# Three feed-forward stages: the down product of the last group of chunks by seven products of half size, and the next norm's blocks in the order in which they are finished

## The chip, the core and the metric

The kernel runs on one core of a Trainium2 chip. The metric is the device time of one execution in microseconds. Time before: 1751.9 us, the median of three runs (1751.84 to 1753.63).

The engines as the profile names them: PE multiplies matrices and accumulates into PSUM, PEld loads its weights, DVE and ACT work elementwise, POOL issues some of the DMAs (those that add to memory on chip among them), and SP issues the loads of the weights. Each engine has one queue of instructions and waits on semaphores of the others.

## The reference

A trunk of two layers on 512 tokens of width 1024, float32. Each layer is a feed-forward net, a mixer (gated linear attention, GLA, in the first layer, stick-breaking attention, SB, in the second) and another feed-forward net, each behind an RMSNorm:

```python
def swiglu(h, w_gate, w_up, w_down):
    return (jax.nn.silu(h @ w_gate) * (h @ w_up)) @ w_down

    for i in range(DEPTH):          # 2
        x = x + 0.5 * swiglu(rmsnorm(x, ffn1_norm[i]), ffn1_w_gate[i], ffn1_w_up[i], ffn1_w_down[i])
        h = rmsnorm(x, mix_norm[i])
...
        x = x + y.astype(x.dtype)
        x = x + 0.5 * swiglu(rmsnorm(x, ffn2_norm[i]), ffn2_w_gate[i], ffn2_w_up[i], ffn2_w_down[i])
    return rmsnorm(x, final_norm)
```

The gate and up matrices are 1024 x 2816, the down matrix is 2816 x 1024. So there are six stages in a row: FFN, GLA, FFN, FFN, SB, FFN, and then the last norm.

## The kernel before

**Layout.** The activations are held transposed: eight tiles `xs[0]` to `xs[7]` of 128 features x 512 tokens (in the traces all of them are `x`, in the order of instructions `x_81` to `x_88`). Float32 products are made of three matmuls: each operand is split into a high part (a cast to fp32r, on ACT) and a low part (the difference, on DVE), and PE adds high x high, low x high and high x low. So every weight block costs a cast (`wh`, L152), a subtraction (`wl`, L153) and, for PE, three matmuls for each pair of blocks. A matmul has 128 x 128 weights and 512 columns (tokens), or 256 where products are of half size.

**Seven products.** From chunk 2 on, gate and up products (`FFN.seven`) split weights and activations into 2 x 2 blocks and compute the product in Winograd's form: seven products of half size for eight, with sums of weight blocks (`sums_12`, `sums_34`, on DVE), sums of activation blocks (`t1` to `t4`) and sums of the results. `seven_down` does the same for the down product of a group of two chunks: the weights are 512 x 1024, taken in two parts; part 0 has the output blocks 0, 1 (lower) and 4, 5 (upper), part 1 the blocks 2, 3 and 6, 7. For each part it loads two blocks of 512 KB (`rawd`, two buffers) and queues two entries. `body_1` makes four products (with `b11`, `t1`, `t2`, `b21`), `body_2` three (`t3`, `b22`, `t4`); each product is 2 x 6 matmuls of 256 columns into the tiles `ps_w`, `ps_z` and `ps_q`. The weight sums `s34` of the second entry are split by `low_34` (casts at L427, low parts at L430). A result is added to half a tile of `xs` as soon as it is there (`add`, L418), three halves' results one over the other, so that `xs` is read and written 12 times in a part. The plain `down` (L334) takes 512 x 256 of the weights in an entry, 24 matmuls of 512 columns, and adds whole tiles (L367).

**Groups.** A stage has eleven chunks of 256 hidden features in six groups: `GROUPS = ((0, 2), (2, 4), (4, 6), (6, 8), (8, 9), (9, 11))`. While the gate and up products of a group run, the down products of the group before are mixed in between: for groups 1 and 3 (`DOWN_SEVEN`) by `seven_down`, its first part behind the first up product, its second part (`late`) some slots later; for the others by `down`. Some blocks of the plain downs are not added by DVE: ACT writes half the result to `d` (L362), and POOL starts a DMA that adds it to `xs` (L363). In group 4 these are six of eight blocks (`HOMES`). The down products of the last group, group 5, stand alone at the end of the stage: this part is called the tail here.

**Hidden values.** When an up product is done, the gated value is closed: `close` casts it whole and takes its low part (`hh`, `hl`); for a group in `DOWN_SEVEN` `close_first` and `close_second` make the halves `b11`, `b21`, `b22` and the four sums `t1` to `t4`, with a cast and a low part for each; places for some are free halves of the normed input `self.n`.

**The next norm.** In the tail each `xs[k]` gets its last sum, and `prep(k)` then makes the next stage's input from it: the high part `xh` (L544, ACT), the low part `xl` (L545, DVE), the square (L535, ACT) and the sum of the squares (L536, DVE). The scale of the norm is put on later, so PE can start the next stage's products on `xh` and `xl` before it is known; `new_norm` says in which order they take the eight blocks.

**What sets the order.** Work is queued as entries (`Feed.q`). An entry's weights are split when it is one of the next three and four tiles of full size are not yet taken; raw blocks are loaded up to six entries ahead, as far as their buffers go. The scheduler then orders each engine's instructions by priority; a queue is worked off in that order.

## Time and profile before

| | |
|---|---|
| median of three runs | 1751.9 us (1751.84 to 1753.63) |
| the profiled execution: time | 1752.18 us |
| the profiled execution: span, first to last instruction | 1750.2 us |
| granted TensorE clock, mean | 0.999 |
| matmuls | 12698 |
| tails of the three stages, PE, us from the span's start | 312.67 to 333.39; 850.83 to 871.55; 1172.27 to 1192.99 |
| weights loaded by SP in one 512 KB block (`rawd`), issue to landing | 3.8 us, median of 84 |

Times in the views are in us from the start of the span. A row of the timeline has the start, the duration, the engine, the line, the operation and its tiles, and then the idle time of the engine before it and what ended it. Rows of a window have, for each engine, the busy time and in brackets how many instructions it touches; then the granted clock, the mean share of the 16 DMA engines and GB/s. A row of the waits has the waiting instruction, what it waited for, the sum, how often, and the longest. Durations of neighbours overlap a little, since an instruction starts before the one before it on its engine has ended; how long a queue takes is read from start to start.

### The profile page before, as it was taken

Reading aid. Unit: us, or ns where it says so; the run is one execution under the profiler, and the core shown is the slowest. Engines: PE = TensorE matmul, PEld = TensorE weight load, DVE = VectorE, ACT = ScalarE, POOL = GpSimd, SP = SyncE. Lnnn points to the kernel's source line nnn. Section 1 sums busy time; section 2 is a strip of 40 time slices with the busy share of each in tenths; the row PEclk is TensorE's granted clock in tenths of the full one; section 3 lists DMA queues with packets and bytes.
Section 4 is the critical chain, followed back from the end, with each engine's and each line's share of the span. In section 5 each row is a group of like instructions: output and inputs, shape, how many; then the busy total and the mean of one; then the engine's idle time right before and its main releaser. Section 6 shows DMA issues by size and latency. Waiting matters only on the chain.

```text
span 1750.2 us, 31332 instructions
## 1 busy us (share of the span) xinstructions
PE 1740.0 (99%) x12698; PEld 1628.1 (93%) x12698; DVE 1507.0 (86%) x2490; ACT 1026.3 (59%) x1832; POOL 55.8 (3%) x85
## 2 busy tenths in 40 slices
PE   9999999999999999999999999999999999999998
PEld 8999999889888899999989999999888889999997
DVE  8999798786888989889799988977999679998886
ACT  7556555554665565555665555555666655565555
POOL 0000000200000000000000000010000000000000
PEclk9999999999999999999999999999999999999999
DMA  5533434412223443444334334343212234434441
GB/s 169 157 109 121 127 116 139 120 55 75 72 75 119 112 129 112 118 129 125 105 125 127 115 118 124 121 111 108 75 59 73 73 97 133 123 107 123 119 140 60
DMA packets 186244, 193.11 MB, mean 110 GB/s; under 512 B 4786, under 2 KB 170980, under 8 KB 186100
## 3 DMA queue, kind: packets, MB, share of 16 engines
q1 hardware_dynamic: 177760, 175.91, 32.3%
q0 software_dynamic: 8096, 14.92, 4.7%
q8 instruction: 99, 1.62, 0.4%
q14 instruction: 45, 0.37, 0.1%
q10 hardware_dynamic: 244, 0.29, 0.0%
HBM read 175.11 MB, written 2.10 MB: 101 GB/s over the span
## 4 chain that ended last, share of the span: by engine, by line
PE 95%; DVE 4%; ACT 1%; issue 0%; DVEq 0%
PE ps_w L779 22%; PE ps_f L80 16%; PE ps_d L80 16%; PE ps_q L779 11%; PE ps_z L779 6%; PE ps_w L412 5%; PE ps_t L80 5%; PE ps_b L80 4%; PE ps_q L412 2%; PE ps_z L412 1%; PE ps_z L1484 1%; PE ps_oT L1546 1%; PE ps_T L1531 1%; PE ps_bt L80 1%; PE ps_S L80 1%; PE ps_o L80 1%
## 5 line engine op out<-in xcount | busy, mean ns | idle before, releaser
L153 DVE TENSOR_TENSOR wl<-raw,wh 128x1024 fp32r<-128x1024 f32 x241 | 255.4, 1060 | 40.5 <-ACT wh L152 39.6
L152 ACT CAST wh<-raw 128x1024 fp32r<-128x1024 f32 x241 | 222.1, 922 | 81.2 <-PE ps_f L80 34.3
L153 DVE TENSOR_TENSOR wl<-s,wh 128x1024 fp32r<-128x1024 f32 x160 | 195.3, 1221 | 66.2 <-ACT wh L152 65.3
L779 PE MATMUL ps_w<-th,wh 128*128 128x256 f32 x864 | 238.8, 276 | 0.0
L779 PE MATMUL ps_w<-tl,wh 128*128 128x256 f32 x864 | 237.6, 275 | 0.0
L779 PE MATMUL ps_w<-th,wl 128*128 128x256 f32 x864 | 237.6, 275 | 0.0
L152 ACT CAST wh<-s 128x1024 fp32r<-128x1024 f32 x160 | 168.7, 1054 | 6.0 <-DVE s L765 6.0
L779 PEld LDWEIGHTS ps_w<-th,wh 128*128 128x128 f32 x864 | 165.8, 192 | 0.5 <-ACT ps_z L807 0.2
L80 PE MATMUL ps_f<-xh,wh 128*128 128x512 f32 x432 | 166.0, 385 | 0.0
L779 PEld LDWEIGHTS ps_w<-tl,wh 128*128 128x128 f32 x864 | 165.9, 192 | 0.0
L779 PEld LDWEIGHTS ps_w<-th,wl 128*128 128x128 f32 x864 | 165.9, 192 | 0.0
L80 PE MATMUL ps_f<-xh,wl 128*128 128x512 f32 x432 | 164.0, 380 | 0.5 <-DVE wl L153 0.5
L80 PE MATMUL ps_f<-xl,wh 128*128 128x512 f32 x432 | 163.8, 379 | 0.0
L80 PE MATMUL ps_d<-hh,wh 128*128 128x512 f32 x416 | 157.8, 379 | 0.0
L80 PE MATMUL ps_d<-hl,wh 128*128 128x512 f32 x416 | 157.7, 379 | 0.0
L80 PE MATMUL ps_d<-hh,wl 128*128 128x512 f32 x416 | 157.7, 379 | 0.0
L153 DVE TENSOR_TENSOR wl<-rawd,wh 128x1024 fp32r<-128x1024 f32 (+1 forms) x100 | 96.2, 962 | 8.6 <-ACT wh L152 8.6
L807 ACT COPY ps_z<-ps_w 128x256 f32<-128x256 f32 x72 | 26.1, 362 | 117.9 <-PE ps_w L779 117.7
L363 POOL DMA_DIRECT2D x<-d x53 | 46.0, 912 | 1525.9 <-ACT d L362 1108.1
L80 PEld LDWEIGHTS ps_f<-xh,wl 128*128 128x128 f32 x432 | 81.8, 189 | 11.4 <-DVE wl L153 0.9
L80 PEld LDWEIGHTS ps_f<-xl,wh 128*128 128x128 f32 x432 | 81.7, 189 | 11.5
L80 PEld LDWEIGHTS ps_f<-xh,wh 128*128 128x128 f32 x432 | 81.7, 189 | 10.7
(355 smaller groups left out, 5355.8 us busy)
## 6 DMA issues: line engine op xcount, KB each, us to landing
raw<-in_ffn_w_gate_dram SPq DMA_DIRECT2D x43, 1024.0 KB, 5.5
raw<-in_ffn_w_up_dram SPq DMA_DIRECT2D x43, 1024.0 KB, 5.4
rawd<-in_ffn_w_down_dram SPq DMA_DIRECT2D x84, 512.0 KB, 3.8
x<-d POOLq DMA_DIRECT2D x53, 256.0 KB, 4.4
raw<-in_gla_w_in_dram SPq DMA_DIRECT2D x12, 1024.0 KB, 5.3
raw<-in_sb_w_in_dram SPq DMA_DIRECT2D x16, 512.0 KB, 3.7
raw<-in_gla_w_out_dram SPq DMA_DIRECT2D x4, 1024.0 KB, 5.0
raw<-in_sb_w_in_dram SPq DMA_DIRECT2D x4, 1024.0 KB, 5.1
```

The costliest lines, as they stand in the source:

```text
L80: st["pe"] = nc.tensor.matmul(ps, l, r, start=first, stop=last).ins
L152: nc.scalar.copy(h[:, k], part)
L153: nc.vector.tensor_tensor(out=l[:, k], in0=part, in1=h[:, k].bitcast(F32), op=ALU.subtract)
L363: nc.gpsimd.dma_start(xs[k], d, accum_op=ALU.add)
L412: st["pe"] = nc.tensor.matmul(ps, l_, r_, start=first and c + n == 0, stop=c == 1 and n == 2, skip_group_check=True).ins
L779: st["pe"] = nc.tensor.matmul(o, l_, r_, start=first and j + n == 0, stop=j == 3 and n == 2, skip_group_check=True).ins
L807: v["copied"] = nc.scalar.copy(z, w).ins
L1484: nc.tensor.matmul(o_, l_, r_, start=first, stop=last, skip_group_check=True)
L1531: nc.tensor.transpose(ps[:, c0 : c0 + P], ys[yb][:, yc + j * P : yc + (j + 1) * P], ident)
L1546: nc.tensor.matmul(po[e * 64 : e * 64 + 64, j * P : T], self.v[j][:, c : c + 64], self.wt[p, e][bk][:, c0 : c0 + n], start=j == 0, stop=j ...
```

## The change

In the three feed-forward stages that are not the last, group 5 joins groups 1 and 3: its down product is made by `seven_down`, both parts directly behind each other at the end of the stage. Its two chunks are closed by `close_first` and `close_second`; for the second, the sums `t3` and `t4` get a whole tile of the normed input. `seven_down` has a new argument `nxt`: behind the last add to a block it calls `prep` for it. Blocks are finished in the order 0, 1, 4, 5, 2, 3, 6, 7, and the next stage's products take them in this order (`st["order"]`). The second part of group 3's `seven_down` moves from the second to the first slot of group 5, where it stood behind the first up product and now stands behind the first gate product. The last stage keeps its old form.

```diff
-    def seven_down(pool, w, r0, hs, part):
+    def seven_down(pool, w, r0, hs, part, nxt=None):
...
             for m in range(2):
                 add(m, 0, 1, flat(qs[m]))
+                if nxt is not None:
+                    nxt(part * 2 + m)
             yield
             for m in range(2):
                 prod(ws[m], v["a2"], 2, m, "t4", False)
                 add(m, 1, 0, flat(ws[m]))
+                if nxt is not None:
+                    nxt(part * 2 + m + 4)
             yield
...
     def new_norm():
-        st["h"], st["l"], st["made"] = st["nh"], st["nl"], range(KD)
+        st["h"], st["l"], st["made"] = st["nh"], st["nl"], st.pop("order", range(KD))
...
-        DOWN_SEVEN = (1, 3)
+        DOWN_SEVEN = (1, 3, 5)
...
             self.gi, self.normed = gi, False
+            self.down_seven = self.DOWN_SEVEN[: 2 if last else 3]
...
-                    if group - 1 in self.DOWN_SEVEN and i == 1:
+                    if group - 1 in self.down_seven and i == 1:
                         args = (lambda: self.tp, wd, self.GROUPS[group - 1][0] * 256, self.hs[group - 1])
                         seven_down(*args, 0)
 
-                        late.append((0 if slots > 2 else 1, (*args, 1)))
+                        late.append((1 if last and slots == 2 else 0, (*args, 1)))
...
             if last:
                 back_tok(wd, c0 * 256, n, self.hs[group], nxt)
             else:
-                for x in downs:
-                    down(*x)
+                for part in range(2):
+                    seven_down(lambda: self.tp, wd, c0 * 256, self.hs[group], part, nxt)
...
-            if len(self.hs[group]) == 1:
+            if group + 1 == len(self.GROUPS) and len(self.hs[group]) == 2:
+                h, l = self.cut(*self.n[4], ts[:, 2:4].rearrange("p a b -> p (a b)"))
+                b["t3"], b["t4"] = (h[:, 0:H], l[:, 0:H]), (h[:, H:T], l[:, H:T])
+            elif len(self.hs[group]) == 1:
...
                 feed.entries(self.total - self.count)
+                if len(self.down_seven) > 2:
+                    st["order"] = (0, 1, 4, 5, 2, 3, 6, 7)
```

Behind line 483 the lines of the changed kernel are two to ten higher than before (`prep`'s L545 is L549, L536 is L540).

How the tail of the first stage stands in the queues, first on DVE. Before, behind the first downs of group 5: `ps_d` is a down's result, `wl<-raw` the low part of the next stage's weights, `xl` and `ss` are the next norm's.

```order
L367 SCALAR_TENSOR_TENSOR x_82<-ps_d,x_82 128x512
L153 TENSOR_TENSOR wl<-raw,wh 128x1024
L545 SCALAR_TENSOR_TENSOR xl<-x_82,gT,xh 128x512
L536 TENSOR_TENSOR ss<-ss,sq 128x512
L367 SCALAR_TENSOR_TENSOR x_83<-ps_d,x_83 128x512
L545 SCALAR_TENSOR_TENSOR xl<-x_83,gT,xh 128x512
L536 TENSOR_TENSOR ss<-ss,sq 128x512
L367 SCALAR_TENSOR_TENSOR x_84<-ps_d,x_84 128x512
L153 TENSOR_TENSOR wl<-raw,wh 128x1024
L545 SCALAR_TENSOR_TENSOR xl<-x_84,gT,xh 128x512
```

Of the change, the same place of DVE's queue from the first add of part 0 on; `s_3852` is part 0's s34, `s_3917` and `s_3960` are part 1's s12 and s34.

```order
L418 SCALAR_TENSOR_TENSOR x_85<-ps_q,x_85 128x256
L396 TENSOR_TENSOR s_3917<-rawd 128x512
L403 TENSOR_TENSOR s_3960<-rawd 128x512
L397 TENSOR_TENSOR s_3917<-s_3917,rawd 128x512
L418 SCALAR_TENSOR_TENSOR x_86<-ps_q,x_86 128x256
L404 TENSOR_TENSOR s_3960<-rawd,s_3917 128x512
L430 TENSOR_TENSOR wl<-s_3852,wh 128x512
L418 SCALAR_TENSOR_TENSOR x_81<-ps_w,x_81 128x256
L418 SCALAR_TENSOR_TENSOR x_82<-ps_w,x_82 128x256
L430 TENSOR_TENSOR wl<-s_3852,wh 128x512
L418 SCALAR_TENSOR_TENSOR x_81<-ps_z,x_81 128x256
L418 SCALAR_TENSOR_TENSOR x_82<-ps_z,x_82 128x256
```

Where one add, a low part and the norm's rows stood for each block, part 1's weight sums and part 0's low parts now stand between adds of half the size. Behind this piece follow four low parts of part 1's weights (three of 128x512, one of 128x1024), six more adds of part 0 and one `xl`, and then, still of the change and on DVE, the rows up to the low parts of part 1's s34:

```order
L418 SCALAR_TENSOR_TENSOR x_83<-ps_w,x_83 128x256
L549 SCALAR_TENSOR_TENSOR xl<-x_82,gT,xh 128x512
L540 TENSOR_TENSOR ss<-ss,sq 128x512
L549 SCALAR_TENSOR_TENSOR xl<-x_85,gT,xh 128x512
L549 SCALAR_TENSOR_TENSOR xl<-x_86,gT,xh 128x512
L540 TENSOR_TENSOR ss<-ss,sq 128x512
L418 SCALAR_TENSOR_TENSOR x_87<-ps_q,x_87 128x256
L418 SCALAR_TENSOR_TENSOR x_88<-ps_q,x_88 128x256
L430 TENSOR_TENSOR wl<-s_3960,wh 128x512
L418 SCALAR_TENSOR_TENSOR x_84<-ps_w,x_84 128x256
L540 TENSOR_TENSOR ss<-ss,sq 128x512
L430 TENSOR_TENSOR wl<-s_3960,wh 128x512
```

The norm's rows of part 0's blocks came between the adds of part 1, ahead of the low parts of s34 that part 1's second entry reads.

PE at the end of the stage. Before, the last matmuls of the down product and the first of the next stage (`ps_f`):

```order
L80 MATMUL ps_d<-hh,wh 128x512
L80 MATMUL ps_d<-hh,wl 128x512
L80 MATMUL ps_d<-hl,wh 128x512
L80 MATMUL ps_f<-xh,wh 128x512
L80 MATMUL ps_f<-xh,wl 128x512
```

Of the change, on PE, the start of part 1's second entry (`ps_w` is the product with t3, `ps_q` the one with b22):

```order
L412 MATMUL ps_w<-nh,wh 128x256
L412 MATMUL ps_q<-hh,wh 128x256
L80 MATMUL ps_f<-xh,wh 128x512
L412 MATMUL ps_w<-nh,wl 128x256
L412 MATMUL ps_w<-nl,wh 128x256
L412 MATMUL ps_w<-nh,wh 128x256
```

A matmul of the next stage, which stood behind the whole tail, now stands inside part 1's second entry; a second one follows twelve rows behind it.

More of the change, by code (lines that the diff above doesn't have):

```diff
@@ L743, in __init__ @@
                 ]
-                if group in self.DOWN_SEVEN:
+                if group in self.down_seven:
                     downs = []
@@ L853, in close_0 @@
             def close_0(o0):
-                if group in self.DOWN_SEVEN:
+                if group in self.down_seven:
                     self.close_first(o0, group)
@@ L859, in close_1 @@
             def close_1(o0, o1):
-                if group in self.DOWN_SEVEN:
+                if group in self.down_seven:
                     self.close_second(o0, o1, group)
```

## The prediction

> **What bounds the kernel now.** I read the page first, then TensorE's waits, then windows of the tail of a feed-forward stage.
>
> ```profile
> span 1750.2 us, 31332 instructions
> PE 1740.0 (99%) x12698; PEld 1628.1 (93%) x12698; DVE 1507.0 (86%) x2490; ACT 1026.3 (59%) x1832; POOL 55.8 (3%) x85
> PE 95%; DVE 4%; ACT 1%; issue 0%; DVEq 0%
> ```
>
> 95% of the chain that ended last lies on PE. A busy PE may still be one that waits, so the next view lists what PE waited for in the whole execution.
>
> ```profile
> PE ps_f L80 <- DVE wl L153: 1.0, 2, 0.5
> PE ps_f L1757 <- DVE gT L72: 0.9, 1, 0.9
> PE ps_kd L1259 <- DVE kd L1248: 0.5, 1, 0.5
> PE ps_S L80 <- DVE st L1281: 0.2, 1, 0.2
> PE ps_b L80 <- DVE wl L153: 0.2, 1, 0.2
> PE ps_b L80 <- ACT w L1426: 0.2, 1, 0.2
> ```
>
> These are 3.0 us in all, and none is at L412 or at ps_d. So fewer matmuls shorten the kernel by their whole length, as long as the other engines feed PE in time; and a wait that is added on PE lengthens it by its whole length, since nothing later is idle to take it back.
>
> **What the change removes from PE.** The third and fourth rows of what follows are all engines' work, used below; the first two are windows on PE's products of one kind: the last 120 of L80 into ps_d in the first stage, and one half (part) of a seven-product down.
>
> ```profile
> 307.50:333.39 25.89, 25.89 (x120) 22.49 (x120) 5.17 (x8) 1.56 (x3) 1.00 0.49 122
> 274.17:283.55 9.38, 9.38 (x84) 9.35 (x84) 1.00 0.34 115
> 283.50:307.50 24.00, 24.00 (x195) 23.36 (x195) 15.83 (x25) 12.79 (x23) 2.58 (x3) 1.00 0.65 173
> 307.50:333.40 25.90, 25.90 (x123) 22.68 (x122) 20.72 (x28) 15.34 (x23) 10.29 (x18) 1.00 0.49 122
> ```
>
> A matmul of 512 columns takes 25.89 / 120 = 0.216 us of PE, one of 256 takes 9.38 / 84 = 0.1117 us, which is a little over half. The four down entries of the last group are 4 x 24 = 96 matmuls, 20.72 us (312.67 to 333.39); in their place stand 2 x 84 = 168 of half size, 18.76 us. PE saves 1.96 us in a stage, 5.9 us in three. [...]
>
> **What it adds on DVE.** DVE's own rows at the existing seven-product down (start, duration):
>
> ```profile
> 277.50 0.74 DVE L418 SCALAR_TENSOR_TENSOR x<-ps_q,x 128x256 f32<-128x256 f32 x2
> 278.17 0.68 DVE L430 TENSOR_TENSOR wl<-s,wh 128x512 fp32r<-128x512 f32 x1
> 278.76 0.75 DVE L418 SCALAR_TENSOR_TENSOR x<-ps_w,x 128x256 f32<-128x256 f32 x2
> 282.43 1.22 DVE L153 TENSOR_TENSOR wl<-s,wh 128x1024 fp32r<-128x1024 f32 x1
> 283.56 0.75 DVE L418 SCALAR_TENSOR_TENSOR x<-u,x 128x256 f32<-128x256 f32 x2
> ```
>
> and in the tail, where the next norm's blocks are made:
>
> ```profile
> 320.27 0.75 DVE L545 SCALAR_TENSOR_TENSOR xl<-x,gT,xh 128x512 fp32r<-128x512 f32 x1
> 320.94 0.68 DVE L536 TENSOR_TENSOR ss<-ss,sq 128x512 f32<-128x512 f32 x1
> 321.54 0.69 DVE L367 SCALAR_TENSOR_TENSOR x<-ps_d,x 128x512 f32<-128x512 f32 x1
> ```
>
> From start to start in a full queue: 0.335 us for 128x256 (0.67 for two), 0.60 for 128x512, 1.13 for 128x1024, 0.67 for xl. A stage gains 24 adds of 256 for 8 of 512 (+3.2 us), 8 sums of 512 (+4.8), low parts of 2 x (0.6 + 1.13 + 1.2 + 1.2) for 4 x 1.13 (+3.7), and in the close of two chunks 2 x (5 x 0.335 + 3 x 0.60) for 4 x 0.60 (+4.6): 16.3 us. By the two windows of all engines above, DVE idles 24.0 - 15.83 + 25.9 - 20.72 = 13.3 us from 283.5 to 333.4. The cover is smaller than the work, and most of the work cannot move ahead: adds wait for products, sums for loads.
>
> The downs of group 3 that move one slot earlier I cost at nothing: a whole up product (9.4 us) and then a down of 5.2 us lie between them and the tail, and DVE's rows there keep their number.
>
> **The tail step by step.** I walk along DVE's queue of the changed program with these durations, in the first stage's times. Three rows more fix its start:
>
> ```profile
> 302.14 1.22 DVE L153 TENSOR_TENSOR wl<-rawd,wh 128x1024 fp32r<-128x1024 f32 x1
> 311.68 2.63 POOL L363 DMA_DIRECT2D x<-d  x3 [22.29 <-ACT d L362]
> rawd<-in_ffn_w_down_dram SPq DMA_DIRECT2D x84, 512.0 KB, 3.8
> x<-d POOLq DMA_DIRECT2D x53, 256.0 KB, 4.4
> ```
>
> 1. rawd has two buffers, and part 0 needs both of its loads before its sums. The second goes out when the row at 302.14 ends (303.36) and lands at 303.36 + 3.8 = 307.2. Behind it DVE has six rows of 512, three of 256 and one of 1024: 5.7 us, so part 0's weights are used up at about 312.9, and only then do part 1's two loads go out. They land between 316.7 and some 318.1 (the second queues behind the first; that end is my estimate from the 3.8).
> 2. PE starts part 0 at 312.67 and ends its second product at 312.67 + 24 x 0.1117 = 315.35. The first add goes to x_85, into which POOL's DMA adds as well: 311.68 + 4.4 = 316.1. So the add starts at 316.1, not at 315.35.
> 3. From that add to the second low part of part 1's s34 (the last row of the second DVE piece of the order) DVE's queue holds 16 adds of 256 (5.36 us), 14 rows of 512 (8.40), one of 1024 (1.13) and four xl (2.68): 17.6 us. PE's product b22 of part 1 needs that last row. Without any wait: 316.1 + 17.6 = 333.7.
> 4. Waits inside it: part 1's sums stand directly behind the first add, and wait for the loads of 1. (316.45 to some 317.7: 1.3 us); the xl rows wait for ACT, where xh takes 0.72 us behind sq and a copy of ps_z (0.4 us, estimated from the next row). So 335.4.
>
> ```profile
> 319.00 0.72 ACT L544 ACTIVATE xh<-x,gT 128x512 fp32r<-128x512 f32 x1
> ```
>
> 5. Behind it PE has 11 + 5 + 6 matmuls of 256: 2.5 us, so it ends the tail at 337.9. Two matmuls of the next stage were done in the stall (0.43 us): 337.4, against 333.39 before. **Each stage loses about 4.0 us** where PE alone would have won 1.96. With no wait of step 4 the loss is 2.3 us; with two more waits of the size of step 1's load (1 to 1.5 us each) it is 6.5.
>
> That PE uses blocks 0, 1, 4, 5 first I cost at nothing: it starts 24 of its next matmuls (5.2 us) while the other four blocks are made. DVE ends those about 10 us behind step 4's row, at 345.4, that is 7.5 us behind PE's end, where before it was
>
> ```profile
> 337.85 0.69 DVE L536 TENSOR_TENSOR ss<-ss,sq 128x512 f32<-128x512 f32 x1
> 884.00:898.00 14.00, 14.00 (x67) 12.26 (x66) 14.00 (x27) 8.18 (x12) 0.00 (x0) 1.00 0.00 1
> 908.46 0.48 PE L80 MATMUL ps_f<-nh,wl 128*128 128x512 f32 x1
> ```
>
> 338.5 - 333.4 = 5.1 us. In the second stage, which another feed-forward stage follows, DVE has no idle time after it (14.00 of 14 us) and PE gets a low part at 908.46 just in time (0.48 us for 0.38). There the 2.4 us more turn into 0 to 2.4 us of waiting; I take 1.3, the middle, since part of the chain to the norm's scale is latency that shifts. The two other stages are followed by mixers with idle time on DVE: nothing.
>
> Sum: 3 x 4.0 + 1.3 = 13.3 us. The profiled execution took 1752.18 us (span 1750.2 and 2.0 around it): 1765.5. The median of the runs, 1751.9, is 0.3 below it: **1765 us**.
>
> **Rivals.**
> - *The queue is not the limit, and PE wins.* 1751.9 - 5.9 = 1746. For it: PE has hidden DVE's lag at both seven-product downs of before, where the adds ran up to 3 us late. Against: there a whole entry of other work followed; here b22 of part 1 must not wait, so step 3's last row would have to end at 312.67 + 9.38 + 60 x 0.1117 = 328.8. That is 12.7 us behind 316.1 for 17.6 us of work. It decides from there: 28% shorter rows, or as many moved behind. 6%.
> - *About even:* half of the queue is hidden, each stage loses what it wins: 1750 to 1754. 6%.
> - *The loads land early and ACT is in time:* only the 2.3 us of step 5: 1751.9 + 6.9 = 1759, perhaps with the 1.3. 18%.
> - *Small rows pay their whole duration.* If in this queue with its many waits each row takes what its record says (0.42, 0.68, 1.22, 0.75), step 3 is 16 x 0.42 + 14 x 0.68 + 1.22 + 4 x 0.75 = 20.5 us, 2.9 more in each stage: 1774. Against: the quoted rows start before their predecessor's end. [...] 10%.
> - *PE's early products of the next stage hold the tail.* PE takes in order; the two ps_f matmuls pulled into the tail wait for weight casts on ACT that stand behind four squares and casts. If a cast is 1 to 2 us late, and the second stage's scale also: 1775 to 1780. 6%.
>
> **How the numbers follow.** The forecast with its own range (1760 to 1771) has 54%. The range 1757 to 1775 takes in the early loads and the full durations: 82%. It leaves out even and faster, and the worst case. A measurement of this kernel tells some 0.2% (3.5 us) from no change. Faster by more: 6%; within: 6%; slower by more: 88%.
>
> **What would show it.** Right: in the changed profile PE's waits name x at L418 or wl at L430 in front of ps_q and ps_w at L412, 3 to 6 us in each of three tails; DVE without idle time there, but for a wait for rawd behind the first add; part 1's rawd issued near 312.9 and the first x_85 add near 316; the next stage's first ps_f near 337. Wrong at step 3: no PE wait at L412. Wrong at step 1 or 4: DVE's wait for rawd under 0.5 us or over 3. Wrong in the last term: the FFN behind the second stage without a wait, or with more than 3 us of it.

## The result, and the profile after

The changed kernel takes 1790.8 us, median of five runs (1790.1 to 1791.0), against 1751.8: 2.19% slower (ratio 1.0219, 95% interval 1.0205 to 1.0234). The forecast was 1765 with a range up to 1775: the sign was right, the size, 39 us for 13, was not. The profiled execution has a span of 1788.4 us, 38.2 more than before. The page of the changed kernel, the span, the busy times and the chain:

```profile
span 1788.4 us, 31960 instructions
PE 1751.0 (98%) x12914; PEld 1639.7 (92%) x12914; DVE 1555.5 (87%) x2625; ACT 1048.0 (59%) x1895; POOL 56.3 (3%) x85
PE 72%; DVE 17%; ACT 5%; DMA 4%; issue 2%; DVEq 0%; POOL 0%; SPq 0%; ACTq 0%
```

DVE is busy for 48.5 us more (16.2 in each of the three stages; 16.3 were forecast), and PE has 216 matmuls more, 3 x (168 - 96). The chain that ended last is no longer PE's: 28% of it are DVE, ACT, DMA and issue. What PE waited for, in the whole execution:

```profile
PE ps_q L412 <- DVE x L418: 10.1, 5, 2.5
PE ps_w L412 <- DVE x L418: 8.4, 6, 2.2
PE ps_f L80 <- DVE wl L153: 3.1, 5, 1.0
PE ps_f L80 <- ACT wh L152: 2.2, 1, 2.2
PE ps_w L412 <- ACT ps_z L443: 1.4, 3, 0.5
```

18.5 us stand at L412 behind x adds. In the three tails there are 13.4 of them (4.3, 3.6 and 5.5 us; the forecast had 3 to 6 in each); the other 5.1 stand at group 3, where the forecast had none. Together they are less than the loss. Where it arose shows in the time at which PE starts the first `seven` product of each feed-forward stage (L779 before, L784 after):

| PE starts, us | stage 1 | stage 2 | stage 3 | last stage | end |
|---|---|---|---|---|---|
| before | 64.5 | 602.7 | 923.9 | 1471.9 | 1750.2 |
| after | 64.5 | 614.9 | 952.1 | 1509.4 | 1788.4 |
| later by | 0 | 12.2 | 28.2 | 37.5 | 38.2 |
| lost in the stage and the start behind it | 12.2 | 16.0 | 9.3 | 0.7 | |

The stage that loses most, 16.0 us, is the one that another feed-forward stage follows. Within stage 1, PE is 2.4 us late when the tail starts (315.1 for 312.7), so a part was lost at group 3. In stages 2 and 3 as much again is lost ahead of the tail, 2.8 and 2.3 us (the tails start at 865.8 and 1202.7, that is 15.0 and 30.4 us later than before, and 12.2 and 28.2 us of that were there at the stage's first `seven` product). DVE's timeline of the changed kernel there:

```profile
251.31 0.69 DVE L396 TENSOR_TENSOR s<-rawd 128x512 f32<-128x512 f32 x1 [2.43 <-DMA rawd<-in_ffn_w_down_dram]
251.91 0.75 DVE L418 SCALAR_TENSOR_TENSOR x<-ps_q,x 128x256 f32<-128x256 f32 x2
```

The weight sum of the part that was moved one slot forward waits 2.43 us for its load, and the additions of the part before it stand behind it: the last matmul of their product starts at 248.62, they start at 251.91, 0.60 us behind the sum. The tail's first stall, on the same queue, and the two issues that it waits for (SP and POOL):

```profile
320.39 0.42 DVE L418 SCALAR_TENSOR_TENSOR x<-ps_q,x 128x256 f32<-128x256 f32 x1 [1.54 <-DMA x<-d]
321.74 0.69 DVE L396 TENSOR_TENSOR s<-rawd 128x512 f32<-128x512 f32 x1 [0.93 <-DMA rawd<-in_ffn_w_down_dram]
...
324.49 0.68 DVE L430 TENSOR_TENSOR wl<-s,wh 128x512 fp32r<-128x512 f32 x1
...
340.54 0.69 DVE L430 TENSOR_TENSOR wl<-s,wh 128x512 fp32r<-128x512 f32 x1
```

```profile
314.52 0.97 SPq L108 DMA_DIRECT2D rawd<-in_ffn_w_down_dram  x2
```

```profile
314.32 2.64 POOL L363 DMA_DIRECT2D x<-d  x3 [22.04 <-ACT d L362]
```

The loads go out at 314.5 and 315.1 and the sum starts at 321.74. POOL's adding transfers go out at the same time and need 6 us for the first addition. Both lots are on the queues together (medians of this window of the trace, 312 to 324):

```profile
rawd<-in_ffn_w_down_dram SPq DMA_DIRECT2D x2, 512.0 KB, 5.5
x<-d POOLq DMA_DIRECT2D x3, 256.0 KB, 8.1
```

Then there is something of which the prediction has no word. Windows of the changed kernel, cut where the record of the granted clock changes (the number behind the instruction counts is the clock; the first number in each row is the window's length, the next PE's busy time):

```profile
251.98:255.39 3.41, 1.65 (x15) 1.68 (x16) 3.41 (x10) 0.53 (x3) 0.00 (x0) 1.00 0.01 2
320.24:323.66 3.42, 1.36 (x13) 1.17 (x11) 2.35 (x5) 0.00 (x0) 0.00 (x0) 1.00 1.05 223
323.66:330.48 6.82, 5.50 (x24) 5.21 (x25) 6.82 (x14) 2.83 (x5) 0.00 (x0) 0.50 0.01 3
337.31:340.72 3.41, 1.91 (x12) 1.54 (x12) 3.41 (x8) 3.41 (x7) 0.00 (x0) 1.00 0.00 0
340.72:344.14 3.42, 3.42 (x17) 3.33 (x16) 3.42 (x6) 0.76 (x3) 2.79 (x5) 0.50 0.15 28
873.20:876.61 3.41, 0.78 (x4) 0.60 (x5) 3.29 (x8) 2.09 (x3) 0.00 (x0) 1.00 0.22 38
876.61:880.03 3.42, 3.42 (x18) 3.42 (x17) 3.42 (x7) 0.75 (x2) 0.00 (x0) 0.50 0.00 0
...
890.27:893.68 3.41, 3.31 (x14) 3.23 (x15) 3.41 (x8) 1.23 (x3) 0.00 (x0) 0.50 0.02 5
...
1224.78:1228.19 3.41, 3.26 (x15) 3.20 (x15) 3.41 (x8) 1.94 (x4) 0.00 (x0) 0.50 0.02 5
```

Behind stalls PE's clock is halved (0.50) for 3.41 or 6.82 us. In the three tails that is 6.83 + 4 x 3.41 = 20.5 us at half clock, so up to 10.2 us lost again behind the stalls themselves; before, the clock was whole until the last 3.3 us of the kernel. All these stretches start a multiple of 3.413 us from each other (1224.78 is 264 times that behind 323.66); a trace cut at these distances gives the grid of windows that is meant below. None of the windows ahead of the stretches is idle: there are 0.78 to 1.91 us of PE's work in them.

Not every stall has this price. The third tail begins with the same two stalls as the second (2.2 and 1.2 us for 2.5 and 1.2), but there they fall into two windows of the grid, and both are followed by full clock:

```profile
1207.71:1211.12 3.41, 1.53 (x14) 1.34 (x12) 2.42 (x5) 0.06 (x1) 0.00 (x0) 1.00 1.04 223
1211.12:1214.54 3.42, 1.97 (x15) 1.78 (x16) 3.42 (x9) 2.40 (x4) 0.00 (x0) 1.00 0.00 0
```

The window ahead of the stretch at 340.72, on the other hand, holds no stall longer than 0.92 us (two, of 0.58 and 0.92).

### The profile page after: what moved, and what is told of

Its sections match the earlier page's. It is cut to its first block, busy times and chain, and to the rows that moved or that the text cites. A ratio compares the mean times of both kernels' runs of the same rounds, so it can differ in the third digit from the quotient of the medians.

```text
span 1788.4 us, 31960 instructions
## 1 busy us (share of the span) xinstructions
PE 1751.0 (98%) x12914; PEld 1639.7 (92%) x12914; DVE 1555.5 (87%) x2625; ACT 1048.0 (59%) x1895; POOL 56.3 (3%) x85
## 3 DMA queue, kind: packets, MB, share of 16 engines
q8 instruction: 101, 1.65, 0.4%
## 4 chain that ended last, share of the span: by engine, by line
PE 72%; DVE 17%; ACT 5%; DMA 4%; issue 2%; DVEq 0%; POOL 0%; SPq 0%; ACTq 0%
PE ps_w L784 15%; PE ps_f L80 13%; PE ps_d L80 9%; PE ps_q L784 7%; PE ps_w L412 5%; DVE wl L153 5%; PE ps_t L80 5%; PE ps_z L784 3%; PE ps_b L80 3%; PE ps_q L412 3%; DMA rawd<-in_ffn_w_down_dram 2%; ACT wh L152 2%; PE ps_z L1494 1%; DMA raw<-in_ffn_w_gate_dram 1%; PE ps_oT L1556 1%
## 5 line engine op out<-in xcount | busy, mean ns | idle before, releaser
L153 DVE TENSOR_TENSOR wl<-s,wh 128x1024 fp32r<-128x1024 f32 x166 | 202.8, 1222 | 59.2 <-ACT wh L152 58.8
L784 PE MATMUL ps_w<-th,wh 128*128 128x256 f32 x864 | 239.0, 277 | 1.2 <-ACT o L821 1.0
L784 PE MATMUL ps_w<-th,wl 128*128 128x256 f32 x864 | 237.6, 275 | 0.0
L784 PE MATMUL ps_w<-tl,wh 128*128 128x256 f32 x864 | 237.6, 275 | 0.0
L152 ACT CAST wh<-s 128x1024 fp32r<-128x1024 f32 x166 | 175.0, 1054 | 25.6 <-DVE s L397 19.6
L784 PEld LDWEIGHTS ps_w<-th,wh 128*128 128x128 f32 x864 | 165.8, 192 | 2.8 <-ACT o L821 1.8
L784 PEld LDWEIGHTS ps_w<-tl,wh 128*128 128x128 f32 x864 | 165.9, 192 | 0.0
L784 PEld LDWEIGHTS ps_w<-th,wl 128*128 128x128 f32 x864 | 165.8, 192 | 0.0
L80 PE MATMUL ps_d<-hh,wh 128*128 128x512 f32 x320 | 121.3, 380 | 0.5 <-ACT wh L152 0.5
L80 PE MATMUL ps_d<-hh,wl 128*128 128x512 f32 x320 | 121.3, 379 | 0.0
L80 PE MATMUL ps_d<-hl,wh 128*128 128x512 f32 x320 | 121.3, 379 | 0.0
L153 DVE TENSOR_TENSOR wl<-rawd,wh 128x512 fp32r<-128x512 f32 (+1 forms) x106 | 93.2, 887 | 0.0
```

What stands on the lines that cost most here:

```text
L80: st["pe"] = nc.tensor.matmul(ps, l, r, start=first, stop=last).ins
L152: nc.scalar.copy(h[:, k], part)
L153: nc.vector.tensor_tensor(out=l[:, k], in0=part, in1=h[:, k].bitcast(F32), op=ALU.subtract)
L784: st["pe"] = nc.tensor.matmul(o, l_, r_, start=first and j + n == 0, stop=j == 3 and n == 2, skip_group_check=True).ins
```

## Experiments

Times are medians of four runs, each with the kernel before beside it on the same chip (1751.8 to 1752.5). An interval of a ratio is about 0.0015 wide to each side, 2.6 us, so differences of two kernels under about 4 us settle nothing. In the order of the questions; the table at the end has all of them.

**1. The slot in group 3.** Of the change, only this, in the kernel before (`slot_only`), and the opposite, the changed kernel without it (`no_slot`):

```diff
-                        late.append((0 if slots > 2 else 1, (*args, 1)))
+                        late.append((1 if last and slots == 2 else 0, (*args, 1)))
```

> The kernel before, with one thing of the change: in the three stages that are not last, the second part of group 3's seven products is put in slot 0 instead of 1. Theory (in slot 0 the first weight sum of that part, which waits for a load that is late, comes ahead of the first part's x additions in VectorE's queue): about 5.7 us slower than before, 1757.5 (1756 to 1759), with a TensorE gap of 1.5 to 2.5 us in each of the three group 3 places, as at 251.3 in the changed kernel. Rival (the slot costs only together with the new tail): 1751.8, within 1 us.

> The changed kernel with the slot of group 3's second part put back to what it was. Theory (slot and tail cost apart from each other): 1790.8 - 5.7 = 1785 (1783.5 to 1786.5), the gap at 251.3 gone and the three tails as they were. Rival (the stall only moves on to the next late load): 1789 to 1792.

`slot_only` takes 1759.5 us, 7.6 more than before (ratio 1.0044, 1.0027 to 1.0060): the slot costs without the new tail, so the step that costed it at nothing was wrong by itself. Its first place pays twice, once for the wait and once for the clock (windows of `slot_only`):

```profile
251.67:255.08 3.41, 1.40 (x12) 1.43 (x13) 3.41 (x10) 0.85 (x2) 0.00 (x0) 1.00 0.01 2
255.08:258.49 3.41, 3.41 (x18) 3.41 (x17) 3.41 (x5) 0.37 (x1) 0.00 (x0) 0.50 0.00 0
```

`no_slot` computes something else: the closing of group 5's first chunk writes halves of the normed input that group 3's second part still has to read as its own, so that part multiplies other values, as many as before. By the code, that is why the slot moves with the change. Its time, 1792.5 us, isn't lower (1.0232, 1.0217 to 1.0247): the rival held, the stall moved on. Not to a late load, though. DVE's timeline of `no_slot`, where the part now stands:

```profile
276.01 0.69 DVE L893 TENSOR_TENSOR hl<-o,hh 128x512 fp32r<-128x512 f32 x1
...
278.82 0.69 DVE L770 TENSOR_TENSOR s<-s,raw 128x512 f32<-128x512 f32 x1
279.42 0.76 DVE L418 SCALAR_TENSOR_TENSOR x<-ps_q,x 128x256 f32<-128x256 f32 x2
```

The additions come at 279.4, where they came at 277.5 before (the prediction's row): ahead of them now stand nine rows that close group 5's chunk in halves and sums (L893, L968), where two stood before (L888).

**2. The queue at group 3.** The sums that wait are held behind the first part's low parts (`hold_g3`; the held entries are opened, and their sums, casts and low parts ordered, behind the last L430 row):

```diff
                 low_34(2, added)
+            for e in v.get("held", ()):
+                e.open, e.sums_behind = True, v.get("low", added)
+                e.casts_behind = v.get("low", added)
...
                         seven_down(*late.pop()[1])
+                        if not last and group == 5:
+                            for e in feed.q[-2:]:
+                                e.open, e.held = False, True
+                            v0["held"] = feed.q[-2:]
```

> The changed kernel; in group 3 of the three stages (not in the tails) the second part's sums are held behind the first part's low parts. Theory (slot 0 costs because the sum that waits for a late load stands ahead of additions that TensorE waits for): the gap of 2.2 us at 251 goes, the two later ones too, 1785 (1783.5 to 1787). Rival (the load is late wherever its reader stands, as in no_slot: the gap only moves to the second part, near 267): 1789 to 1792.

1786.2 us, 4.6 less than the changed kernel (1.0191, 1.0176 to 1.0206). The additions no longer wait (timeline of `hold_g3`):

```profile
249.86 0.76 DVE L419 SCALAR_TENSOR_TENSOR x<-ps_q,x 128x256 f32<-128x256 f32 x2
250.53 0.68 DVE L431 TENSOR_TENSOR wl<-s,wh 128x512 fp32r<-128x512 f32 x1
```

The load is as slow as it was (median from issue to landing 4.7 us in the window 243 to 256, 4.9 in the changed kernel); that its reader stood ahead of others was the cost.

**3. The same in the tails, and the adding transfers.** `hold_sums` holds the second part's sums in the tails; `hold_homes` also holds that part's casts and low parts, and lets DVE update blocks 4 and 5, which the tail adds to first, instead of POOL. POOL takes block 7 in exchange, so that DVE has one addition of 0.6 us more in each stage, not the 1.2 us that the expectations name:

```diff
-                if m < len(homes):
+                if len(homes) == 3 and part:
+                    home = (None, None, "d", "ss")[m]
+                else:
+                    home = homes[m] if m < len(homes) else None
+                if home is not None:
```

> The changed kernel; in the three tails the weight sums of the second part are held until the first part's last low part is done, so that a late load stands in nobody's way; no work is added or taken. Theory A (position in VectorE's queue): the first low part comes at about 321.5 instead of 324.5, the first stall of each tail (2.7 and 1.5 us) shrinks to under 2 us and the half clock behind it goes with it: 3 to 5 us per tail, 1776 to 1782. Theory B (VectorE's work is the bound of the tail, only its idle 1.4 us per tail can be won): 1786 to 1789. Rival (the second part's sums, now later still, stall its first products for as long): 1790 or more.

> The changed kernel; in the three tails the second part's sums and low parts are held behind the first part's low parts (as in hold_sums), and two of the x blocks that the tail adds to first (4 and 5) are no longer updated by an accumulating transfer of POOL but by VectorE. hold_sums kept a first stall of 3 to 4 us, and its second x addition stood at 322.2, behind the transfer of block 5 (issued 314.8). Theory (the accumulating transfers, 6 to 7.5 us from issue to landing, are what holds the first part): the first stall shrinks under 1 us, no half clock behind it, 3 to 5 us per tail less than hold_sums' 1792.8: 1778 to 1784. Rival (VectorE's total work is the bound, and it rises by 1.2 us per tail): 1789 to 1794.

`hold_sums` took 1792.8 us: no gain, theory A fell. Its timeline says why; behind the sums stood a second wait, for POOL's transfers:

```profile
319.65 0.42 DVE L418 SCALAR_TENSOR_TENSOR x<-ps_q,x 128x256 f32<-128x256 f32 x1 [1.40 <-DMA x<-d]
322.23 0.42 DVE L418 SCALAR_TENSOR_TENSOR x<-ps_q,x 128x256 f32<-128x256 f32 x1 [2.15 <-DMA x<-d]
```

With both away, `hold_homes` took 1783.3 us, 7.5 less than the change, although DVE does a little more: its work as such was not yet the bound. With `hold_g3` added the two gains add up:

> hold_homes and hold_g3 together. Theory (both are waits of VectorE's in-order queue, at separate places, and add up): hold_homes 1783.3 - 5.7 - 1.2 (the half clock that hold_homes had after the gap at 251) = 1776 to 1778. Rival (the late loads catch up with the kernel elsewhere): 1781 to 1784.

`hold_all`: 1776.0 us, as the theory said. PE's longest wait in it is again one for DVE:

```profile
PE ps_q L417 <- DVE x L423: 5.7, 4, 2.8
```

**4. The load itself.** `raw_bufs` loads the tail's second part into the ring of the gate and up weights, which is free earlier:

```diff
-        lower.few = upper.few = True
+        lower.few = upper.few = nxt is None or part == 0
```

> The changed kernel; in the three tails the second part's down weights are loaded into the ring of the gate and up weights (free by about 305), not into the ring that is full until 313; the next stage's first weights come later for it. Theory (the late load is what stalls the tails): VectorE makes the sums while it was idle (from 318), the first stall shrinks to what the accumulating transfer of block 4 and 5 leaves (x additions at 320.4 and 322), 2 to 4 us per tail, 1779 to 1785. Rival (those transfers alone hold the first part, so the load's time is covered): 1787 to 1791. Rival (the next stage waits for its weights): above 1791.

This one line brings 14.5 us, the most of all single edits: 1776.3 (1.0147, 1.0129 to 1.0165), more than the theory asked. DVE's timeline of `raw_bufs` at the start of the tail, and the transfers in its window from 311 to 323:

```profile
316.59 0.68 DVE L396 TENSOR_TENSOR s<-raw 128x512 f32<-128x512 f32 x1
...
319.59 0.68 DVE L404 TENSOR_TENSOR s<-raw,s 128x512 f32<-128x512 f32 x1
320.20 0.74 DVE L418 SCALAR_TENSOR_TENSOR x<-ps_q,x 128x256 f32<-128x256 f32 x2
320.86 0.68 DVE L430 TENSOR_TENSOR wl<-s,wh 128x512 fp32r<-128x512 f32 x1
```

```profile
x<-d POOLq DMA_DIRECT2D x3, 256.0 KB, 4.3
```

The sums, 2.4 us of work, fill time in which DVE was idle. The adding transfers land after 4.3 us instead of 8.1, with no load beside them, and the additions no longer wait for them either. The first low part starts at 320.86 instead of 324.49 (6.9 us behind the start of the tail, which here is at 314.0, instead of 9.4), and of five stretches at half clock in the tails two are left.

**5. The clock by itself.** `fill12` adds 12 matmuls to each part of the three tails, into the half of the `ps_w` tiles that nothing reads, ahead of the stalls:

```diff
                 prod(ws[m], s, 2, m, "t2", False)
+                if nxt is not None:
+                    bh = turns(hs[1]["b21"][0])
+                    for _ in range((12, 12)[part] // 2):
+                        nc.tensor.matmul(more[m], v["a2"][0][:, 0, 0:P], bh, start=False, stop=True, skip_group_check=True)
```

> The changed kernel with 12 more half-size matmuls in each part of the three tails (72 in all, about 8 us of TensorE work) ahead of the places where TensorE stalls; they write half a PSUM bank that nothing reads. Theory (the half clock after a stall is a cost of its own: 20.5 us of the three tails ran at half clock): the half-clock stretches go or shrink, the stalls shrink by what is filled, and the kernel is faster although it does more: 1781 to 1786. Rival (VectorE sets the pace of the tail whatever the clock): 1790 to 1793. Rival (the fillers only add): up to 1798.

1785.5 us, 5.3 less than the change with 8 us more work on PE (1.0194, 1.0179 to 1.0209). The three tails of `fill12` in windows, from the first product of the tail to the next stage's first:

```profile
316.30:343.10 26.80, 23.30 (x196) 22.33 (x195) 24.31 (x48) 16.11 (x29) 5.07 (x8) 1.00 0.30 72
863.00:890.30 27.30, 23.50 (x195) 22.36 (x194) 24.48 (x49) 17.52 (x30) 1.94 (x3) 1.00 0.40 106
1196.60:1223.80 27.20, 23.12 (x195) 22.07 (x194) 24.75 (x49) 15.57 (x30) 3.28 (x12) 1.00 0.29 68
```

The clock is whole in all three, and they take 81.3 us together. In the changed kernel they take 88.7, cut in the same way:

```profile
315.10:345.50 30.40, 25.03 (x172) 23.67 (x171) 26.11 (x52) 16.12 (x29) 6.55 (x12) 0.83 0.29 66
865.80:896.10 30.30, 23.91 (x172) 22.76 (x171) 25.96 (x52) 17.48 (x30) 1.75 (x2) 0.89 0.37 96
1202.70:1230.70 28.00, 21.86 (x170) 20.88 (x169) 25.54 (x52) 15.19 (x28) 2.74 (x12) 0.94 0.31 73
```

The half clock was a cost of its own. `fill12` is a measurement, no remedy: `all_fill`, with hold_homes, late_preps and the fillers, gained nothing over it.

> The changed kernel with hold_homes, late_preps and fill12 together: 8 us of matmuls more that nothing reads, VectorE's queue in the order in which TensorE waits for it, no accumulating transfer ahead of the tail's first additions. Theory (queue order and the clock are the whole of what the tails lose beyond VectorE's own work): 1766 to 1775. Rival (VectorE's work of about 20 us per tail stays the bound): 1780 to 1786, no better than fill12.

1785.3 us; the theory fell. In its trace PE waits only 0.4 us for x in the three tails, so the fillers there have hardly a stall left to fill and stand on the path for the most part; that this is why it gains nothing is read from the trace, and was not tried apart.

**6. DVE's work and its order.** `late_preps` makes the next norm's pieces of the first part's blocks behind the second part's low parts:

```diff
+            for k in norms:
+                with behind(v.get("low", added)):
+                    nxt(k)
...
-                    seven_down(lambda: self.tp, wd, c0 * 256, self.hs[group], part, nxt)
+                    seven_down(lambda: self.tp, wd, c0 * 256, self.hs[group], part, nxt if part else norms.append, norms if part else ())
```

> The changed kernel; in the three tails the next norm's pieces for the first part's four blocks (4 rows of 0.75 us and the sums of squares) are made behind the second part's low parts instead of ahead of them. Theory (VectorE's queue is full from 322 to 342 in the tail, and the 4 us of norm pieces in it stand ahead of rows that TensorE waits for): the second stall of each tail (0.9 and 1.3 us) goes, and the half clock behind it (3.4 us at half speed, 1.7 lost): 2 to 3 us per tail, 1782 to 1785. Rival (the norm pieces are then what the next stage's first products wait for): 1789 to 1793.

> raw_bufs, with the blocks 4 and 5 updated by VectorE (as in hold_homes) and the sums held in group 3 (as in hold_g3). Theory (late load and late accumulating transfer are all that the tails lose beyond VectorE's work): the waits of 1.5 to 3.6 us for the second part's first sums go, and the half clock behind them, 2 to 3 us per tail below hold_all's 1776.0: 1766 to 1771. Rival (VectorE's work is what is left): 1774.5 to 1778.

> raw_bufs, with the sums held in group 3 (hold_g3) and the first part's norm pieces behind the second part's low parts (late_preps); blocks 4 and 5 as in the change. In raw_all VectorE worked without a pause from 312 to 340 and TensorE waited 2 to 3 us per tail (0.9 and 1.0, 2.1, 2.1), each time while four norm pieces and two sums of squares (331.4 to 327.4 and what follows) stood ahead of the second part's additions and low parts. Theory (once the loads are early, the order in VectorE's full queue is what is left): 1.5 to 3 us per tail below raw_all's 1775.0, and 1.2 us of VectorE's work less: 1766 to 1771. Rival (as in late_preps, what is won in the tail is lost at the next stage's start): 1773 to 1777.

By itself, `late_preps` took 1790.8 us: nothing. `raw_all`, with early loads and without adding transfers on blocks 4 and 5, took 1775.0, no less than `hold_all` or `raw_bufs`: the rival held. There, in the first tail, DVE has no idle time left worth the name (window of `raw_all`; DVE is the third busy time):

```profile
312.40:340.00 27.60, 23.58 (x177) 22.29 (x176) 27.09 (x55) 17.64 (x32) 6.09 (x10) 0.94 0.41 107
```

`raw_late` took 1770.7, 4.3 less (1.0105, 1.0088 to 1.0121). That the order counts in this state isn't shown by it: it differs from `raw_all` in two things, the late norm pieces and blocks 4 and 5, which POOL keeps (0.6 us less for DVE in each tail), and from `raw_bufs`, 5.6 us slower, by `hold_g3`, which brought 4.6 by itself, and the late norm pieces. Its waits of PE:

```profile
PE ps_f L80 <- DVE wl L154: 3.7, 5, 1.4
PE ps_d L80 <- ACT wh L152: 2.1, 2, 1.2
PE ps_f L80 <- ACT wh L152: 1.8, 1, 1.8
PE ps_w L413 <- DVE x L419: 1.7, 3, 0.6
```

Of the 13.4 us of waiting for x at the tails' products 2.8 are left (1.7 and 1.1 for `ps_q`), and none of the 5.1 at group 3. The other waits in this view stand behind the tails, at the next stage's products.

**7. The stage that a feed-forward stage follows.** `raw_no_ffn` and `raw_late_no_ffn` leave the change out there. Of their edit the line that decides it; the slot and the plain `down` in the tail go with it:

```diff
-            self.down_seven = self.DOWN_SEVEN[: 2 if last else 3]
+            self.down_seven = self.DOWN_SEVEN[: 2 if last or len(phases) == 2 else 3]
```

> raw_all, with the second of the three stages, the one that a feed-forward stage follows, as it was before the change (tail, slot and order). Theory (what that tail and the start after it lose, 9 to 12 us in hold_all against before, is theirs alone): 9 to 11 us below raw_all, about 1757 to 1761; still slower than before, since TensorE wins 2 us per tail and VectorE's queue costs more. Rival (the loss comes back elsewhere): under 4 us below raw_all.

> raw_late with the second stage as before the change: the version in which everything that helped is together. Theory: two tails gain 1.5 to 3 us each over raw_no_ffn's 1763.4: 1757 to 1760, 5 to 8 us slower than before. Rival (no gain): 1762 to 1765. Faster than before (below 1750) is expected by none of them: it would need more than the 2 us of TensorE work that a tail saves.

1763.4 and 1762.2 us. The first is 11.6 below `raw_all`, a little more than the 9 to 11 of the theory (its 1757 to 1761 counted on a faster `raw_all`): what that stage loses is its own. Between the two no difference can be measured, so here the rival held, and no pair of runs shows a gain by the late norm pieces alone. The second is the lowest of all, and 0.56% slower than before (1.0056, 1.0041 to 1.0071). The same table as above, for the two kernels with late norm pieces, counted from the first `seven` product of stage 1 (which starts at 64.7 and 64.3 us, for 64.5 before):

| PE later than before, us | stage 1 | stage 2 | stage 3 | last stage | span |
|---|---|---|---|---|---|
| lost in the stage, `raw_late` | 3.6 | 11.5 | 3.6 | 0.6 | 1769.9 |
| lost in the stage, `raw_late_no_ffn` | 3.8 | 0.6 | 3.2 | 0.4 | 1758.0 |

Most of what stage 2 of `raw_late` loses is lost behind its tail, which takes 21.3 us (856.0 to 877.3). From there to 940 PE waits 5.3 us, 3.9 for casts of ACT and 1.4 for a low part of DVE, and runs at half clock for two stretches of 3.41 us, from 880.43 and from 911.15.

**8. The order of the blocks, and early products.**

> The changed kernel with the next norm's blocks taken in the order 0 to 7 instead of 0, 1, 4, 5, 2, 3, 6, 7. Prediction on record: costs and brings nothing, 1790.8 within 1.5 us. Rival (the next stage's products meet blocks 2 and 3, finished last, in third and fourth place instead of fifth and sixth, and wait): up to 2 us per tail, 1793 to 1797.

> The changed kernel; the next stage's first products are kept behind the tail's last product in TensorE's queue. In the profile of the changed kernel the early product of block 0 held TensorE for 2.2 us at 887.4 in the second tail, with half clock behind it, and none in the first tail. Theory (a rival of the prediction: early products hold the tail, but only in one tail of three): 2 to 4 us less, 1787 to 1789. Rival (without them the tail's own waits take the same time): 1790 to 1793.

With the default order 1792.5 us (1.0231, 1.0216 to 1.0246): 1.7 us above the change, where 1.5 were allowed for; the intervals overlap, so nothing measurable, as the prediction had it. With the next stage's first products kept behind the tail, 1791.4: nothing either, though the wait of 2.2 us for the early product (the fourth line of the waits of the changed kernel) was there; in its place the tail's own product waits 2.5 us for x, up to 891.74. The same in two other settings:

> hold_all and psf_behind together. hold_homes still waited 2.5 us at 879.4 in the second tail for the early product of block 0. Theory: 2 to 4 us below hold_all, 1772 to 1776. Rival: as hold_all, within 1.5 us. By either, slower than before, because the start of the stage after the second tail and VectorE's added work stay.

> raw_all and psf_behind together. Theory (early products of the next stage still stand in the tail, in the second one above all): 1 to 3 us below raw_all. Rival: within 1 us of it.

1775.1 us beside 1776.0, and 1776.2 beside 1775.0: no effect that can be told from none.

| kernel | us | ratio to before |
|---|---|---|
| the change | 1790.8 | 1.0219 |
| slot_only (kernel before + slot) | 1759.5 | 1.0044 |
| no_slot | 1792.5 | 1.0232 |
| hold_sums / hold_homes | 1792.8 / 1783.3 | 1.0235 / 1.0178 |
| hold_g3 / hold_all | 1786.2 / 1776.0 | 1.0191 / 1.0134 |
| raw_bufs / raw_all | 1776.3 / 1775.0 | 1.0147 / 1.0131 |
| fill12 / all_fill | 1785.5 / 1785.3 | 1.0194 / 1.0186 |
| late_preps / raw_late | 1790.8 / 1770.7 | 1.0220 / 1.0105 |
| raw_no_ffn / raw_late_no_ffn | 1763.4 / 1762.2 | 1.0067 / 1.0056 |
| order_default / psf_behind | 1792.5 / 1791.4 | 1.0231 / 1.0221 |
| hold_all_psf / raw_all_psf | 1775.1 / 1776.2 | 1.0130 / 1.0140 |

## Why the prediction was right in sign and wrong in size

- **PE's matmuls, DVE's added work:** right. 72 more matmuls a stage, 16.2 us of DVE work a stage for 16.3 forecast, and too little idle time under it. No version that was run gets below before.
- **"The downs of group 3 that move one slot earlier I cost at nothing": wrong.** 7.6 us in `slot_only`, 7.5 in the three stages of the changed kernel (2.4, 2.8 and 2.3), 4.6 won back by `hold_g3`. The step counted DVE's rows and found as many as before; it did not ask in which order they stand and that the first of them waits for a load.
- **Step 1, the late loads: right in kind, and the step that cost most.** The loads go out when the rows that read their buffers are done: the second at 315.1, at the start of the tail; 0.2 us behind it by the forecast (312.9 with a tail from 312.67). But the sum that needs it starts at 321.74, 6.6 us later, where the forecast had 3.8 to 5.2. The sum took medians of the whole execution (3.8 for `rawd`, 4.4 for `x<-d`); in this window, where the step itself puts both lots on the queues together, they are 5.5 and 8.1. `raw_bufs` took the lateness away, and with it 14.5 us of the 25.8 by which the result missed the forecast.
- **Step 2, the first addition:** 316.1 forecast, 3.4 us behind the start of the tail; 320.39 measured, 5.3 behind it. The same cause.
- **Steps 3 and 4, the queue:** from the first addition to the last row of the second low part 19.3 us forecast (17.6 and 1.7 of waits), 20.8 measured (320.39 to 341.23). Small rows start at each other's heels as the forecast had it (two additions at 338.34 with 0.75 us and a low part at 339.00 with 0.68 are followed 0.66 and 0.60 us after their start); the rival with whole durations isn't what happened. What came on top were waits for a PE and an ACT that were late themselves.
- **Step 5, the end:** 2.5 us forecast for PE's last products, 2.0 less the two early matmuls; 4.3 measured in the first tail (341.2 to 345.5). Three of the five stretches at half clock (those at 340.72, 890.27 and 1224.78) lie on them. The forecast put the clock at full speed without saying so. A term for it belonged behind the waits, and the waits were in the forecast.
- **The start behind the second stage:** 1.3 us forecast, 2.4 at most. The second stage lost 16.0, 3.8 more than the first. With the tails cleared in `raw_late` it lost 11.5, where the two others lost 3.6: 7.9 more, beside the 5.3 us of waits and the two stretches at half clock named above. The mechanism was the one named as far as the traces show it (in `raw_late` DVE works without a pause from 896.6 to 911.1, and PE waits for the low part at the end of it), the size was not: it was taken from the shift of one row, not from the 16.3 us of work less the idle time, and without the clock.
- **3.6 us in each stage that a mixer follows, with early loads and ordered rows:** close to the 4.0 that the forecast had for the change as it stands, but by luck. The forecast put the 4.0 into the tail and nothing behind it; the first tail of `raw_late` takes 21.9 us (312.8 to 334.7), 1.2 more than before, and the rest of the 3.6 is lost behind it.
- **Order of the blocks at nothing:** right. **Early products hold the tail (6%):** the wait is there in one tail, and keeping them behind changes nothing.

By place the loss can be read from the two traces. The tails took 20.72 us each before and take 30.4, 30.3 and 28.0 now.

| loss against before, us | forecast | measured |
|---|---|---|
| ahead of the tails, where group 3's part moved | 0 | 7.5 |
| in the three tails | 12.0 | 26.5 |
| at the start behind the second stage | 1.3 | 3.6 |
| elsewhere, with the last stage | 0 | 0.6 |
| sum | 13.3 | 38.2 |

So the steps that failed are three: the slot costed at nothing, the tail priced at 4.0 us for 7.3 to 9.7, and the start behind the second stage. In the first tail the excess of 5.7 us is 1.9 at the first addition, 1.5 in the queue and 2.3 at the end. By cause the excess can only be said roughly, since the parts are not independent: `raw_bufs` wins 14.5 us by the load and what hangs on it, stalls and half clock together, and `fill12` wins 5.3, with the clock whole in the tails, while it adds 8 us of work. What the last 3.6 us a stage are made of was not tried apart; that they are DVE's work is argued from its full windows.

## What to carry to other kernels

A row that waited for a load (2.43 us at 251.31) held the additions behind it in its engine's queue: when a step is moved forward, look at what its first row waits for and who stands behind it, not only at how many rows there are. Take the time of a transfer from the window in which it will run, with what the change itself starts beside it, not from the median of the execution (5.5 us for 3.8 and 8.1 for 4.4 here). And stalls of one or two microseconds on PE can have a price behind them (20.5 us at half clock in the three tails here): look at the granted clock, window by window, before adding up waits.

## What the runs showed of the hardware

- **Short stalls were followed by half clock.** 3.41 us windows with 0.78 to 1.91 us of PE work in them were followed by one or two at half clock. There is no clean limit in these rows: 1.65 us of work at 251.98 kept the clock, 1.65 at 331.32 in `hold_all`, 1.40 at 251.67 in `slot_only` and 1.91 at 337.31 did not. The trace of the changed kernel, cut by its grid, the first 20 us and the last 10 left out: behind full clock, the four windows with 0.78 to 1.36 us of PE work were followed by half clock, one of the four with 1.53 to 1.91, and none of the 500 with 1.96 or more. So it counts how a stall falls in the grid of windows, and equal stalls cost different amounts, as in the second and third tail of the changed kernel (2.5 and 1.2 us with half clock behind them, 2.2 and 1.2 without).
- **Idle matmuls can pay.** 72 matmuls without a use (8 us) made the changed kernel 5.3 us faster where it stalled, and gained nothing in `all_fill`, where the stalls for x in the tails were gone.
- **Loads and adding transfers took longer beside each other.** The transfers of 256 KB that add to memory on chip landed after 8.1 us beside two loads, after 4.3 without them (`raw_bufs`); the two loads beside them took 5.5 us, two loads without them 4.9 (243 to 256 in the changed kernel), and the median of the kernel before is 3.8.
